# Where plain fp32 products give way to split ones in the up projection of a mixture-of-experts kernel

## The chip, the cores and the metric

The kernel runs on one core of a Trainium2 chip. The metric is the device time of one execution in microseconds. Three executions took 1799.08, 1800.51 and 1802.31 us; their median is 1800.51 us. The profiled execution took 1802.38 us, of which the span from the first to the last instruction is 1800.6 us.

## The reference

The reference is one transformer block over 512 tokens of width 1024: a normalisation, one wide input projection, windowed attention, an RWKV7 recurrence, an output projection, and then the part that matters here, a feed-forward layer with 16384 experts ("PEER"). Each token picks 16 experts in each of 8 heads; the two factors of an expert's number are found by top-16 searches over 128 keys each.

```python
idx = jnp.take_along_axis(cidx, pos, axis=-1)
gate = jax.nn.softmax(top, axis=-1)
def expert_block(args):
    xc, ic, gc = args
    hpre = jnp.einsum('ckd,cd->ck', u_tab[ic], xc).astype(f32)
    act = jax.nn.gelu(hpre, approximate=False) * gc
    return jnp.einsum('ck,ckd->cd', act.astype(v_tab.dtype), v_tab[ic])
```

## The kernel before, in words

For three quarters of the tokens (`TD` = 384) the kernel does not gather experts. It runs all 16384 of them densely, in 128 steps of 128 experts: an up step multiplies the 1024 x 128 slice of the table `u_t` with the 384 normalised tokens and takes the GELU, a matrix of gates (zero for experts that were not picked) is multiplied on, and a down step multiplies with `v_t`. The last 128 tokens gather their rows instead. Matrices are fp32. A product of fp32 accuracy is made in one of two ways. The split way (`mm3`, lines 95 to 98) keeps each operand as a high part of type fp32r and a low part, the rest, and issues three TensorE products: low x high, high x low, high x high. The plain way issues one product of fp32 type, which the trace records as two PE instructions.

The parts of the weights come from `weights` (lines 128 to 141): a DMA on SP's queue into one of `RAWB` = 4 buffers `wraw`, a copy to fp32r on ScalarE (line 139) into `wh` or `wxh`, and a subtraction that gives the low part `wl` or `wxl` on the engine in `lo` (line 140). Each of the four names has two buffers. For the up steps here `lo` is GpSimd (POOL), since `LOP` and `LOQ` are both 4.

The first 42 up steps (`AHEAD`) do not stand in the main loop. They fill TensorE while the top-16 searches and the gates are made, in the function `window`. There PE and VectorE (DVE) follow an order written out by hand; ACT, POOL and SP are ordered by the framework's planner. DVE makes, for each of 48 groups of 8 tokens, one-hot matrices (`onehots`, line 556, output `ot`, 5 buffers) and gated ones (lines 562 and 564, `hi` and `ot`; in every third group ACT does the second of these, line 568), and between the groups pieces of the top-16 search (MAX8, FIND_INDEX8, MATCH_REPLACE8 and small operations, lines 654 to 756). PE makes the gates of a group two groups behind (`gates`, line 581), which frees that group's `ot`. Between the groups PE takes "units" of up steps: `U(n)` advances by `n` of the eight k-parts of a step. 12 units (`RES`) are held back until after the last gates. Then the main loop begins: down step e beside up step e + 42.

An up step has eight k-parts of 128 rows. In the first `PLAIN` steps the parts 0 to 3 are split and the parts 4 to 7 are plain: the raw weights are read by PE directly from `wraw`, against `x2f`, the unsplit tokens, which `whole` builds once in the four buffers of `wxh` and `wxl`. After that all parts are split, and `wxh` and `wxl` carry weights.

```python
def u_prep(e):
    if e < PLAIN:
        U[e] = [weights(a["u_t"][e][:, :4], lo=G)]
        with tc.high_priority(offset=PRE):
            U[e].append(ws.tile([P, 4, P], F32, name="wraw", bufs=RAWB))
            nc.sync.dma_start(U[e][1], a["u_t"][e][:, 4:])
        return
    odd[0] = True
    U[e] = [weights(a["u_t"][e][:, h * 4:h * 4 + 4], lo=G if e <= AHEAD and (2 * e + h) % LOP < LOQ else V) for h in range(2)]
...
            if e < PLAIN and k >= 4:
                PE.matmul(o, uu[1][:, k % 4], x2f[k][:, :TD], start=False, stop=k == KD - 1)
            else:
                uh, ul = uu[k // 4]
                mm3(o, uh[:, k % 4], ul[:, k % 4], x2h[:, k, :TD], x2l[:, k, :TD], k == 0, k == KD - 1)
```

Of the kernel before, what the change touches and what calls it, by code (L numbers as in the profile page):

```python
# [43 lines left out]
AHEAD = 42  # L44
# [6 lines left out]
UN0 = ((14, (1,)), (14, (1,)), (14, (1,)), (14, ()))  # L51
NG8 = TD // 8
GSC = 2.0 ** 15
PLAIN = AHEAD - 2
GB2 = 2
LAG = 2
RES = 12
# [251 lines left out]
def peer(tc, a, out, dump, mm3, split, mhalf, ws, ps, weights, x2h, x2l, xg, h1_dram, dram, hb, qst, tst, tk, tk0, scores,  # L309
# [6 lines left out]
    with ExitStack() as st:  # L316
# [15 lines left out]
# [10 lines that stand above are left out]
        def u_mm(e):  # L342
            uu = U.pop(e)
            o = ps.tile([P, TD], F32, name="mm", bufs=2)
            for k in range(KD):
                if e < PLAIN and k >= 4:
                    PE.matmul(o, uu[1][:, k % 4], x2f[k][:, :TD], start=False, stop=k == KD - 1)
# [1114 lines left out]
```

## Time and profile before

| | value |
|---|---|
| median of 3 executions | 1800.51 us (1799.08 to 1802.31) |
| profiled execution | 1802.38 us |
| its span | 1800.6 us |
| mean granted TensorE clock | 0.98 |
| PE busy | 1719.2 us (95%) |
| DVE busy | 1385.5 us (77%) |
| POOL busy | 786.5 us (44%) |
| ACT busy | 716.6 us (40%) |
| up steps ahead, first plain product to last | 628 to 875 us |
| main loop at full TensorE use | from about 912 us |

The shares are means over stages that are bound by different engines; what a change in one stage is worth is read from the waits of that stage. A matmul's recorded duration overlaps the next one's, so its cost is read from the distance between starts. "L140" is line 140 of the kernel; for a helper like `weights` the tile names tell which use is meant.

### The profile page before, as it was taken

Reading aid. Unit: us, or ns where it says so; the run is one execution under the profiler, and the core shown is the slowest. Engines: PE = TensorE matmul, PEld = TensorE weight load, DVE = VectorE, ACT = ScalarE, POOL = GpSimd, SP = SyncE. Lnnn points to the kernel's source line nnn. Section 1 sums busy time; section 2 is a strip of 40 time slices with the busy share of each in tenths; the row PEclk is TensorE's granted clock in tenths of the full one; section 3 lists DMA queues with packets and bytes.
Section 4 is the critical chain, followed back from the end, with each engine's and each line's share of the span. In section 5 each row is a group of like instructions: output and inputs, shape, how many; then the busy total and the mean of one; then the engine's idle time right before and its main releaser. Section 6 shows DMA issues by size and latency. Waiting matters only on the chain. (4 is left out here: it accounts for less than half of the span.)

```text
span 1800.6 us, 30100 instructions
## 1 busy us (share of the span) xinstructions
PE 1719.2 (95%) x10913; PEld 1433.8 (80%) x10913; DVE 1385.5 (77%) x2540; ACT 716.6 (40%) x1540; POOL 786.5 (44%) x642
## 2 busy tenths in 40 slices
PE   7998899999999889999899999999999999999998
PEld 6766666667778867777789999999999999987886
DVE  4666765755435998998769988787888998989896
ACT  4453132221334545766633333334333333333334
POOL 5534332311154522222255555555555655556550
PEclk9998999999999999999999999999999999999999
DMA  6221111111564324455599999999999999989974
GB/s 209 79 66 46 31 42 48 42 48 48 160 216 134 106 82 177 177 208 206 205 307 320 315 329 328 306 327 325 315 314 332 312 316 332 310 301 299 299 237 161
DMA packets 193397, 378.98 MB, mean 210 GB/s; under 512 B 18624, under 2 KB 65472, under 8 KB 190176
## 3 DMA queue, kind: packets, MB, share of 16 engines
q1 hardware_dynamic: 97344, 175.71, 28.7%
q0 software_dynamic: 36864, 134.23, 22.0%
q10 hardware_dynamic: 59040, 67.12, 11.1%
q8 instruction: 85, 1.39, 0.3%
q14 instruction: 64, 0.52, 0.1%
HBM read 342.12 MB, written 33.55 MB: 209 GB/s over the span
## 5 line engine op out<-in xcount | busy, mean ns | idle before, releaser
L140 POOL TENSOR_TENSOR wl<-wraw,wh 128x512 fp32r<-128x512 f32 (+1 forms) x102 | 146.0, 1432 | 352.5 <-ACT wh L139 304.1
L96 PE MATMUL w<-vh,al 128*128 128x512 f32 x663 | 259.5, 391 | 5.6 <-DVE al L102 5.6
L97 PE MATMUL w<-vl,ah 128*128 128x512 f32 x663 | 259.0, 391 | 0.0
L98 PE MATMUL w<-vh,ah 128*128 128x512 f32 x663 | 258.8, 390 | 0.0
L404 POOL DMA_INDIRECT grow<-v_t,idxV x128 | 172.2, 1345 | 181.0 <-DVE gacc L421 157.2
L404 POOL DMA_INDIRECT grow<-u_rows,idxU x128 | 166.6, 1302 | 178.1 <-DVE grow L411 162.3
L357 ACT ACTIVATE big<-mm 128x384 f32<-128x384 f32 x128 | 62.5, 489 | 422.8 <-PE mm L98 339.9
L96 PE MATMUL mm<-x2h,wl 128*128 128x384 f32 (+1 forms) x544 | 194.7, 358 | 16.0 <-ACT big L357 14.6
L140 DVE TENSOR_TENSOR wl<-wraw,wh 128x512 fp32r<-128x512 f32 x96 | 136.2, 1418 | 95.0 <-ACT wh L139 73.0
L98 PE MATMUL mm<-x2h,wh 128*128 128x384 f32 (+1 forms) x544 | 183.1, 337 | 0.0
L97 PE MATMUL mm<-x2l,wh 128*128 128x384 f32 (+1 forms) x544 | 182.9, 336 | 0.0
L139 ACT ACTIVATE wh<-wraw 128x512 fp32r<-128x512 f32 (+1 forms) x198 | 123.6, 624 | 145.2 <-PE mm L776 50.7
L421 DVE SCALAR_TENSOR_TENSOR gacc<-grow,act,gacc 128x1024 f32<-128x1024 f32 x127 | 166.8, 1314 | 2.2
L102 DVE TENSOR_TENSOR vl<-vraw,vh 128x512 fp32r<-128x512 f32 x212 | 143.1, 704 | 19.3 <-ACT vh L101 19.2
L411 DVE SCALAR_TENSOR_TENSOR grow<-grow,xg 128x1024 f32<-128x1024 f32 x128 | 149.9, 1213 | 0.0
L96 PEld LDWEIGHTS w<-vh,al 128*128 128x128 f32 x663 | 124.9, 188 | 31.1 <-DVE al L102 8.0
L98 PEld LDWEIGHTS w<-vh,ah 128*128 128x128 f32 x663 | 124.7, 188 | 26.3
L370 POOL TENSOR_TENSOR big<-big,gt 128x384 f32<-128x384 f32 x128 | 136.2, 1067 | 20.4 <-ACT gt L586 14.7
L97 PEld LDWEIGHTS w<-vl,ah 128*128 128x128 f32 x663 | 124.9, 188 | 22.6
L101 ACT ACTIVATE vh<-vraw 128x512 fp32r<-128x512 f32 x212 | 127.4, 624 | 37.9 <-DMA vraw<-v_t 29.5
L140 POOL TENSOR_TENSOR wxl<-wraw,wxh 128x512 fp32r<-128x512 f32 (+1 forms) x58 | 83.3, 1436 | 131.4 <-ACT wxh L139 119.0
L96 PE MATMUL mm<-x2h,wxl 128*128 128x384 f32 (+1 forms) x384 | 127.3, 331 | 0.0
(404 smaller groups left out, 4088.8 us busy)
## 6 DMA issues: line engine op xcount, KB each, us to landing
wraw<-u_t SPq DMA_DIRECT2D x256, 256.0 KB
vraw<-v_t SPq DMA_DIRECT2D x212, 256.0 KB
g_dram<-stg ACTq DMA_DIRECT2D x24, 1024.0 KB
gt<-g_dram ACTq DMA_DIRECT2D x60, 384.0 KB
wraw<-wz SPq DMA_DIRECT2D x72, 256.0 KB
wraw<-v_t SPq DMA_DIRECT2D x44, 256.0 KB
wraw<-wq SPq DMA_DIRECT2D x32, 256.0 KB
wraw<-wproj SPq DMA_DIRECT2D x16, 256.0 KB
```

What stands on the lines that cost most here:

```text
L96: PE.matmul(o, ll, rh, start=start, stop=False)
L97: PE.matmul(o, lh, rl, start=False, stop=False)
L98: PE.matmul(o, lh, rh, start=False, stop=stop)
L101: S.activation(hi, src, AF.Copy)
L102: V.tensor_sub(lo, src, hi.bitcast(F32))
L139: S.activation(wh[:, :, :m], raw[:, :, :m], AF.Copy)
L140: lo.tensor_sub(wl[:, :, :m], raw[:, :, :m], wh[:, :, :m].bitcast(F32))
L357: S.activation(H[e], o, AF.Gelu)
L370: G.tensor_mul(ht, ht, g[:, :, e % E2B, :])
L404: G.indirect_dma_start(out=r, out_offset=None, in_=src, in_offset=bass.IndirectOffsetOnAxis(ap=idx[:, i:i + 1], axis=0))
L411: V.scalar_tensor_tensor(r, r, 1.0, xg, op0=ALU.mult, op1=ALU.mult, accum_out=hpre[:, s:s + 1])
L421: V.scalar_tensor_tensor(gacc, r, act[:, i:i + 1], gacc, op0=ALU.mult, op1=ALU.add)
```

## The change

The number of up steps with plain products for half of their contraction falls from 40 (`AHEAD - 2`) to 14. Steps 14 to 39 make all eight k-parts split.

```diff
-PLAIN = AHEAD - 2
+PLAIN = 14
```

## Rows read from the trace of the kernel before

**Rows 1.** Busy time by stretch: PE, PEld (weight load), DVE, ACT and POOL in us with the number of instructions, then the granted TensorE clock, the share of the DMA engines, and GB/s. The stretches are up steps 14 to 39, the way into the main loop, and the main loop.

```profile
715.00:875.00 160.00, 154.49 (x1038) 122.06 (x1035) 147.78 (x437) 102.78 (x241) 40.45 (x28) 0.99 0.54 191
875.00:912.00 37.00, 31.69 (x227) 27.13 (x226) 19.57 (x22) 22.39 (x55) 14.09 (x10) 0.91 0.76 259
912.00:1610.00 698.00, 698.00 (x3553) 637.55 (x3552) 594.68 (x772) 257.96 (x514) 386.13 (x316) 1.00 0.93 321
```

**Rows 2.** Who waited for whom between 711 and 888 us: total us, times, longest us.

```profile
ACT wh L139 <- DMA wraw<-u_t: 22.2, 12, 5.3
DVE ot L556 <- PE w L581: 15.2, 6, 5.1
...
PE mm L96 <- ACT big L357: 5.5, 3, 2.8
```

**Rows 3.** DVE in order of time, the one-hot operations that waited (start us, us; the wait before it and what ended it in brackets).

```profile
711.27 1.23 DVE L556 TENSOR_TENSOR ot<-ids,row 128x2048 f16<-128x2048 f16 x1 [5.05 <-PE w L581]
...
739.44 1.23 DVE L556 TENSOR_TENSOR ot<-ids,row 128x2048 f16<-128x2048 f16 x1 [3.29 <-PE w L581]
...
801.82 1.23 DVE L556 TENSOR_TENSOR ot<-ids,row 128x2048 f16<-128x2048 f16 x1 [1.17 <-PE w L581]
...
815.87 1.22 DVE L556 TENSOR_TENSOR ot<-ids,row 128x2048 f16<-128x2048 f16 x1 [1.66 <-PE w L581]
...
830.89 1.22 DVE L556 TENSOR_TENSOR ot<-ids,row 128x2048 f16<-128x2048 f16 x1 [0.44 <-PE w L581]
...
844.73 1.22 DVE L556 TENSOR_TENSOR ot<-ids,row 128x2048 f16<-128x2048 f16 x1 [3.62 <-PE w L581]
```

**Rows 4.** PE in order of time within one up step: the first of six split products in a row, then the first and the last of the four plain products after them (a plain product is recorded as two instructions, x2).

```profile
783.25 0.34 PE L96 MATMUL mm<-x2h,wl 128*128 128x384 f32 x1
...
784.29 0.81 PE L347 MATMUL mm<-wxh,wraw 128*128 128x384 f32 x2
...
786.22 0.81 PE L347 MATMUL mm<-wxl,wraw 128*128 128x384 f32 x2
```

**Rows 5.** All instructions of the line of the plain products: duration ns min/median/max, first and last start.

```profile
L347 PE MATMUL mm<-wxh,wraw x160: 483/486/847, 628.3 to 874.3; 128*128 128x384 f32 x160
...
L347 PE MATMUL mm<-wxl,wraw x160: 485/486/617, 628.9 to 875.0; 128*128 128x384 f32 x160
```

**Rows 6.** ACT in order of time: the GELU that ends up step 13 (the fourteenth of its line).

```profile
714.72 0.47 ACT L357 ACTIVATE big<-mm 128x384 f32<-128x384 f32 x1
```

**Rows 7.** POOL and ACT groups between 711 and 888 us (ACT: 715 to 880): busy us, mean ns of one, idle before and its releaser.

```profile
L140 POOL TENSOR_TENSOR wl<-wraw,wh 128x512 fp32r<-128x512 f32 x27 | 43.5, 1610 | 125.1 <-ACT wh L139 125.1
L140 POOL TENSOR_TENSOR wxl<-wraw,wxh 128x512 fp32r<-128x512 f32 x2 | 4.0, 2002 | 0.0
```

```profile
L139 ACT ACTIVATE wh<-wraw 128x512 fp32r<-128x512 f32 x26 | 16.3, 629 | 26.8 <-DMA wraw<-u_t 20.0 <-PE mm L98 5.0 <-issue 1.7
```

**Rows 8.** DVE groups between 711 and 888 us: busy us, mean ns of one, idle before.

```profile
L556 DVE TENSOR_TENSOR ot<-ids,row 128x2048 f16<-128x2048 f16 x37 | 48.3, 1305 | 15.2 <-PE w L581 15.2
L562 DVE TENSOR_TENSOR hi<-ot,gps 128x1024 f16<-128x1024 f16 x38 | 31.4, 825 | 0.0
L564 DVE TENSOR_TENSOR ot<-ot,gps 128x1024 f16<-128x1024 f16 x26 | 25.7, 987 | 1.0
L723 DVE TENSOR_TENSOR eq<-eq,tfx 128x2048 bf16<-128x2048 bf16 x4 | 6.7, 1672 | 0.3
L662 DVE FIND_INDEX8 ti<-tv,big 128x8 uint32<-128x128 f32 x20 | 5.5, 285 | 0.0
...
L710 DVE TENSOR_TENSOR wd<-sixteen,sh 128x128 uint32<-128x128 uint32 x2 | 1.5, 766 | 0.1
...
L701 DVE TENSOR_TENSOR ge<-gv 128x128 f32<-128x128 f32 x2 | 1.4, 676 | 0.0
```

**Rows 9.** The three heavy DVE lines over the whole span: duration ns min/median/max, first and last start.

```profile
L556 DVE TENSOR_TENSOR ot<-ids,row x48: 1201/1218/2308, 664.9 to 884.2; 128x2048 f16<-128x2048 f16 x48
L562 DVE TENSOR_TENSOR hi<-ot,gps x48: 677/684/1772, 667.1 to 886.7; 128x1024 f16<-128x1024 f16 x48
L564 DVE TENSOR_TENSOR ot<-ot,gps x32: 691/693/1671, 669.6 to 887.4; 128x1024 f16<-128x1024 f16 x32
```

**Rows 10.** POOL and DVE in order of time at two POOL subtractions (741.22 and 729.85 us), and one DVE operation of line 723 with no POOL work beside it.

```profile
741.22 1.27 POOL L140 TENSOR_TENSOR wl<-wraw,wh 128x512 fp32r<-128x512 f32 x1 [3.95 <-ACT wh L139]
```

```profile
741.37 1.67 DVE L564 TENSOR_TENSOR ot<-ot,gps 128x1024 f16<-128x1024 f16 x1
```

```profile
729.85 1.27 POOL L140 TENSOR_TENSOR wl<-wraw,wh 128x512 fp32r<-128x512 f32 x1 [4.32 <-ACT wh L139]
```

```profile
729.84 0.22 DVE L662 FIND_INDEX8 gi<-gv,cand 128x8 uint32<-128x65 f32 x1
```

```profile
750.43 1.22 DVE L723 TENSOR_TENSOR eq<-eq,tfx 128x2048 bf16<-128x2048 bf16 x1
```

**Rows 11.** The end of the stage in order of time: DVE's last gated operation and its next one, PE's last held-back unit and the first down product.

```profile
887.42 0.69 DVE L564 TENSOR_TENSOR ot<-ot,gps 128x1024 f16<-128x1024 f16 x1
897.56 0.56 DVE L102 TENSOR_TENSOR wl<-big,wh 128x384 fp32r<-128x384 f32 x1 [9.45 <-ACT wh L101]
```

```profile
896.47 0.34 PE L98 MATMUL mm<-x2h,wxh 128*128 128x384 f32 x1
898.27 0.47 PE L96 MATMUL w<-wh,wl 128*128 128x512 f32 x1 [1.46 <-DVE wl L102]
```

## The prediction

> **What bounds the kernel now.** I read the busy time by stretch first. In the main loop PE is busy for all of its 698 us [rows 1]: whatever shifts the start of that loop shifts the end of the kernel by as much, and nothing in the change reaches into the loop. So the question is only when the stage before it ends. In the stretch of up steps 14 to 39 two engines are nearly full: PE with 154.5 of 160 us and DVE with 147.8 [rows 1]. The reader should see that neither share settles which one sets the pace.
>
> The waits come next. DVE's only idle time is before the one-hot operation L556, and PE's gate products end it: 15.2 us in six waits [rows 2]. In time order one wait, at 711.27 us, lies before step 14 begins (step 13's GELU is at 714.72 [rows 6]); the five after it make 3.29 + 1.17 + 1.66 + 0.44 + 3.62 = 10.2 us [rows 3]. PE in turn waits 5.5 us for GELUs that stand behind other work in ACT's queue [rows 2]. So today PE is a little slower than DVE, with DVE running ahead until its five `ot` buffers are used up, and DVE has 10.2 us in hand over the whole stretch. After 844.73 DVE never waits again, and PE's last gates follow DVE's last operation, at 887.42 [rows 11]. That is the balance which the change moves, from both sides.
>
> **What it takes from PE.** The six split products from 783.25 to 784.29 take 1.04 / 6 = 0.173 us each, so a split k-part takes 0.520; the plain ones from 784.29 to 786.22 take 1.93 / 3 = 0.643 us each [rows 4]. 320 records at two for a product are 160 products, 40 steps of four [rows 5]; the change turns 26 x 4 = 104 of them. PE gives back 104 x 0.123 = 12.8 us.
>
> The Trainium skill (FP8 and Floating Point Precision, section TensorE Precision Notes) says that a true fp32 product makes four passes over the array. As an estimate from that page, three passes for four would give back a quarter of 0.643 for each product, 16.7 us; the starts in the trace give 12.8, and the measured number stands.
>
> **What it adds.** Each of the 26 steps gets a second conversion on ACT and a second subtraction on POOL. ACT: 26 x 0.629 = 16.4 us [rows 7], on 102.8 busy of 160 [rows 1]. POOL: 26 x 1.61 = 42 us [rows 7], on 40 busy of 160, so POOL itself stays far from full. The DMAs stay: the same 256 KB are loaded by another line. Raw buffers come free after the subtraction instead of after the last plain product, so ACT's 22.2 us of waiting for raw loads [rows 2] can only shrink. `wxh` and `wxl` become free at the end of step 13 instead of 39; the first conversion into them has the four split parts of step 14 (2.1 us) and a group's gates as cover, and one late start would cost 1 to 2 us of PE, which has 12.8 to give.
>
> ACT works in order, and behind an added conversion stand GELUs (they free PE's accumulators) and gate evictions. From below this costs nothing, because PE's gain covers it; from above, all 16.4 us appear in PE, which with 12.8 us returned would be 3.6 us later than now. I take nothing: DVE, as follows, is later than that.
>
> **What POOL's subtraction does to DVE.** This is the term that decides. At 741.22 a POOL subtraction runs 1.27 us, and beside it the L564 operation takes 1.67 us [rows 10] against a median of 0.693 [rows 9]; the one at 729.85 runs beside FIND_INDEX8, which keeps its 0.22 us [rows 10]. Operations with two tensors are held up; searches are not. The longest cases are 2308 - 1218, 1772 - 684 and 1671 - 693 ns [rows 9], so one meeting costs DVE 0.98 to 1.09 us.
>
> How often do they meet? The sums over 711 to 888 us answer without counting [rows 8]: L556 37 x (1.305 - 1.218) = 3.2 us over its median, L562 38 x (0.825 - 0.684) = 5.4, L564 26 x (0.987 - 0.693) = 7.6, L723 4 x (1.672 - 1.22) = 1.8 (its undisturbed 1.22 is in [rows 10]), and L710 and L701, two each, against 0.28 for an undisturbed one (an estimate: 2 x 0.766 less one meeting of 0.98, halved), 2 x 0.49 + 2 x 0.40 = 1.8. Together 19.8 us, and in that stretch POOL made 27 + 2 = 29 such subtractions [rows 7]: 0.68 us of DVE for each. At the same rate the 26 added ones cost DVE 26 x 0.68 = 17.7 us. From below the cost is zero (all fall beside searches), from above 26 x 1.09 = 28.3 (none does). I take 17.7: the added subtractions are of the same shape in the same stretch.
>
> The Trainium skill (SBUF — State Buffer, section Who interferes with whom) says that GpSimd and a DVE operation with two SBUF inputs lock each other out for a whole instruction, and that one-input operations are spared. The second half agrees with the FIND_INDEX8 at 729.84. By the first, as an estimate, a meeting would cost the 1.27 us of a subtraction and the sum would be 22.9 us; the trace shows 0.98 to 1.09, and it decides.
>
> **The sum.** DVE's list of work is unchanged, in its written order. From 711.27 to its last operation it loses its waits (-10.2 us; PE is 12.8 us faster and DVE later, so its buffers will be free) and gains 17.7: it ends 7.5 us later. PE then waits for DVE; its 12.8 us turn into idle time. From DVE's last operation to the first down product at 898.27 there are 10.9 us [rows 11]: the last gates, 12 held-back units, the eviction and gating of step 0. None of that changes, so the main loop starts 7.5 us later. On the profiled execution's 1802.38 us this is 1809.9; that one lies 1.9 above the median of 1800.51, so the prediction is **1808.0 us**. The likeliest case's own range is 1804 to 1813, from 0.53 to 0.87 us a subtraction.
>
> **Rivals.**
> *PE stays the pace, and the kernel is faster.* Place: DVE's waits before L556. If the added subtractions fall mostly beside searches, they cost DVE less than the time that it has in hand. It decides from 10.2 / 26 = 0.39 us a subtraction downward. For it: 729.85; searches stand in blocks. Against it: 0.68 is the mean of 29 of the same kind. At zero cost PE's gain is the limit: at the wait of 739.44 only four steps have passed (26 steps in 160 us), 4 x 0.49 = 2.0 us, and the 6.9 us of DVE's waits behind it go too, 8.9 us in all and 1791.6. At half the threshold, 26 x 0.2 = 5.2 us, the gain is 5.0 and the time 1795.5. The fewer passes of the page on precision named above point this way.
> *They cancel.* Between 0.39 and 0.53 us a subtraction the end moves by 0 to 3.6 us: 1802 in the middle. For it: the planner may release POOL's pairs together, right after an eviction, at times other than now.
> *ACT's queue becomes the bound.* 16.4 us more in an in-order queue that already made PE wait 5.5 us [rows 2], behind operations that wait for a later DVE; the evictions come late, the gates too, and DVE waits for `ot` again. If half of the 16.4 us shows on top of the 7.5, the time is 1816. Against it: PE now has 12.8 + 7.5 us of slack.
>
> **How the numbers follow.** A measurement of this kernel can tell about 0.2%, 3.6 us, from no change. The forecast gets 0.61, ACT's queue 0.07, cancelling 0.19, PE's pace 0.13. That is slower 0.68, same 0.19, faster 0.13. The range must leave out no more than 2 in 10: from 1797, which leaves out most of PE's pace, to 1816, above which ACT's queue or a dearer subtraction would be.
>
> **What would show it.** Right: between up step 14 and the main loop the waits of L556 for PE's gates are gone or nearly so, L556, L562, L564 and L723 together exceed their medians by some 37 us instead of 20, and PE shows 15 us or more of new idle time before gates, ended by `hi` or `ot`; PE's busy time there is lower by some 13 us; the 898.27 of the first down product becomes some 906. Wrong: L556 still waits for PE by several us and the first down product is earlier; or DVE's excess stays near 20 us although POOL made 26 more subtractions; or PE's new idle time ends with ACT's GELU; or the main loop, which should keep its length, changes.

## The result, and the profile after

The changed kernel takes 1813.35 us (median of 6 executions, 1807.38 to 1814.58) beside 1801.49 us for the kernel before on the same chip: a ratio of 1.0063, 95% interval 1.0048 to 1.0079. It is slower by 11.9 us where 7.5 were forecast; a second measurement of the same two kernels, told below, gave 10.6. The medians below are over all executions; two runs, e1 and e7, each have one far longer execution among theirs (2761.64 and 6726.56 us), and without it their medians are 1800.32 and 1815.39 us. The profiled execution of the change took 1813.65 us, its span 1811.9.

The busy time by stretch, with the columns of [rows 1]: up steps 14 to 39, the way into the main loop, and the main loop. The last line is the whole stretch from step 14 to the first down product.

```profile
715.00:875.00 160.00, 139.14 (x1081) 131.09 (x1080) 158.28 (x421) 110.75 (x258) 88.17 (x53) 0.94 0.52 185
875.00:923.00 48.00, 43.25 (x304) 38.45 (x303) 30.61 (x40) 29.00 (x71) 13.74 (x11) 0.88 0.62 221
923.00:1621.00 698.00, 698.00 (x3554) 637.53 (x3553) 591.86 (x772) 258.11 (x514) 386.63 (x317) 1.00 0.93 321
...
713.00:909.00 196.00, 172.28 (x1342) 160.86 (x1339) 184.46 (x453) 135.71 (x319) 95.81 (x58) 0.93 0.52 189
```

The main loop is what it was. DVE, 147.8 of 160 us before [rows 1], is now busy for 158.3: nothing is left to it but its list of work. PE has gone from 154.5 to 139.1. So the pace has passed from PE to DVE.

Who waited for whom between 711 and 898 us, with the columns of [rows 2]:

```profile
PE mm L96 <- ACT big L357: 20.2, 6, 8.9
...
DVE ot L556 <- PE w L581: 4.4, 1, 4.4
...
ACT wh L139 <- DMA wraw<-u_t: 2.4, 1, 2.4
...
PE w L581 <- DVE hi L562: 0.7, 1, 0.7
```

DVE's six waits for PE's gates [rows 2, 3] have become one, and that one lies before step 14. ACT's waits for raw loads before `wh` fell from 22.2 us to 2.4. But PE's new waits end with ACT's GELU (L357), 20.2 us against 5.5 before, and hardly at all with `hi`.

The DVE groups between 711 and 898 us, with the columns of [rows 8], and POOL's subtractions under them, with the columns of [rows 7]:

```profile
L556 DVE TENSOR_TENSOR ot<-ids,row 128x2048 f16<-128x2048 f16 x37 | 54.8, 1481 | 4.4 <-PE w L581 4.4
L562 DVE TENSOR_TENSOR hi<-ot,gps 128x1024 f16<-128x1024 f16 x37 | 35.3, 954 | 0.0
L564 DVE TENSOR_TENSOR ot<-ot,gps 128x1024 f16<-128x1024 f16 x25 | 29.9, 1197 | 1.0
L723 DVE TENSOR_TENSOR eq<-eq,tfx 128x2048 bf16<-128x2048 bf16 x4 | 5.8, 1455 | 0.3
...
L727 DVE TENSOR_TENSOR eq<-eq 128x1024 bf16<-128x1024 bf16 x4 | 4.7, 1172 | 0.1
L712 DVE TENSOR_TENSOR sh<-rg,sh 128x128 uint32<-128x128 uint32 x2 | 2.8, 1407 | 0.1
...
L732 DVE TENSOR_TENSOR ge<-ge,gs 128x128 f32<-128x128 f32 x2 | 1.8, 916 | 0.1
L676 DVE CAST tf<-ti 128x256 bf16<-128x256 uint32 x2 | 1.5, 768 | 0.1
```

```profile
L140 POOL TENSOR_TENSOR wl<-wraw,wh 128x512 fp32r<-128x512 f32 x27 | 48.8, 1808 | 55.2 <-ACT wh L139 55.2
L140 POOL TENSOR_TENSOR wxl<-wraw,wxh 128x512 fp32r<-128x512 f32 x28 | 44.5, 1592 | 30.4 <-ACT wxh L139 30.4
```

Over the medians of [rows 9] the three one-hot lines lose 37 x 0.263 + 37 x 0.270 + 25 x 0.504 = 32.3 us. The other lines, each over its undisturbed length (1.22, 0.692, 0.293, 0.292 and 0.294 us), add 0.9 (L723), 1.9 (L727), 2.2 (L712), 1.2 (L732) and 0.9 (L676). That is 39.4 us in place of 19.8, and POOL made 55 subtractions in place of 29: 0.72 us each. From 713.27 us to the last gated operation 41 DVE operations take over 0.15 us longer than the same operation does undisturbed, and a POOL operation runs beside every one of the 41; in the kernel before it is 20 of 20.

DVE in order of time, where an added subtraction first falls among one-hot operations (the first two, from 716.21 us, run mostly beside searches), and at the end; then POOL in the same microseconds (start, us, and the wait before in brackets):

```profile
713.27 1.22 DVE L556 TENSOR_TENSOR ot<-ids,row 128x2048 f16<-128x2048 f16 x1 [4.43 <-PE w L581]
...
724.04 0.68 DVE L562 TENSOR_TENSOR hi<-ot,gps 128x1024 f16<-128x1024 f16 x1
724.75 1.67 DVE L564 TENSOR_TENSOR ot<-ot,gps 128x1024 f16<-128x1024 f16 x1
726.34 2.31 DVE L556 TENSOR_TENSOR ot<-ids,row 128x2048 f16<-128x2048 f16 x1
728.57 1.77 DVE L562 TENSOR_TENSOR hi<-ot,gps 128x1024 f16<-128x1024 f16 x1
...
898.90 0.69 DVE L564 TENSOR_TENSOR ot<-ot,gps 128x1024 f16<-128x1024 f16 x1
```

```profile
723.35 2.51 POOL L140 TENSOR_TENSOR wxl<-wraw,wxh 128x512 fp32r<-128x512 f32 x1 [1.42 <-ACT wxh L139]
725.83 1.73 POOL L140 TENSOR_TENSOR wl<-wraw,wh 128x512 fp32r<-128x512 f32 x1
728.27 1.52 POOL L140 TENSOR_TENSOR wxl<-wraw,wxh 128x512 fp32r<-128x512 f32 x1 [0.71 <-ACT wxh L139]
```

The two engines now take turns: three DVE operations in a row are 1.67, 2.31 and 1.77 us long instead of 0.69, 1.22 and 0.68, 3.16 us for three subtractions.

From 711.27 to the end of its last gate operation at 888.12 DVE took 176.85 us before, 10.18 of them waits over 0.2 us; from 713.27 to 899.59 it now takes 186.33, with no such wait. So the waits went (-10.2) and the work grew by 19.7 us, 0.76 a subtraction: 9.5 us. The other 2.0 us of the profiled pair lie before step 14, where the two kernels run the same code (713.27 against 711.27); in the second profile of the change the same operation starts at 709.37, so these 2 us are not the change's.

### The profile page after: what moved, and what is told of

The parts are those of the page before. It is cut to its first block, busy times and chain, and to the rows that moved or that the text cites. A ratio compares the mean times of both kernels' runs of the same rounds, so it can differ in the third digit from the quotient of the medians.

```text
span 1811.9 us, 30401 instructions
## 1 busy us (share of the span) xinstructions
PE 1710.3 (94%) x11017; PEld 1447.9 (80%) x11017; DVE 1404.0 (77%) x2540; ACT 728.6 (40%) x1566; POOL 833.3 (46%) x668
## 3 DMA queue, kind: packets, MB, share of 16 engines
q10 hardware_dynamic: 59040, 67.12, 10.9%
## 4 chain that ended last, share of the span: by engine, by line
PE 47%; DVE 2%; issue 1%; ACT 0%; POOL 0%; DVEq 0%; POOLq 0%; ACTq 0%
PE w L97 9%; PE w L96 9%; PE w L98 9%; PE mm L96 7%; PE mm L98 7%; PE mm L97 7%; DVE gacc L421 0%; DVE al L102 0%; ACT w L472 0%; DVE gt L471 0%; DVE vl L102 0%; DVE gt L481 0%; DVE wl L102 0%; DVE wxl L102 0%; POOL frs L478 0%
## 5 line engine op out<-in xcount | busy, mean ns | idle before, releaser
L140 POOL TENSOR_TENSOR wl<-wraw,wh 128x512 fp32r<-128x512 f32 (+1 forms) x102 | 151.4, 1485 | 285.5 <-ACT wh L139 237.6
L357 ACT ACTIVATE big<-mm 128x384 f32<-128x384 f32 x128 | 62.5, 488 | 417.6 <-PE mm L98 355.1
L96 PE MATMUL mm<-x2h,wl 128*128 128x384 f32 (+1 forms) x544 | 190.6, 350 | 31.9 <-ACT big L357 30.5
L140 DVE TENSOR_TENSOR wl<-wraw,wh 128x512 fp32r<-128x512 f32 x96 | 128.9, 1342 | 98.4 <-ACT wh L139 79.8
L140 POOL TENSOR_TENSOR wxl<-wraw,wxh 128x512 fp32r<-128x512 f32 (+1 forms) x84 | 125.0, 1489 | 158.3 <-ACT wxh L139 145.9
L96 PE MATMUL mm<-x2h,wxl 128*128 128x384 f32 (+1 forms) x488 | 163.8, 336 | 0.0
L98 PE MATMUL mm<-x2h,wxh 128*128 128x384 f32 (+1 forms) x488 | 162.1, 332 | 0.0
L97 PE MATMUL mm<-x2l,wxh 128*128 128x384 f32 (+1 forms) x488 | 162.1, 332 | 0.0
L102 DVE TENSOR_TENSOR vl<-vraw,vh 128x512 fp32r<-128x512 f32 x212 | 144.9, 713 | 21.2 <-ACT vh L101 19.7
L139 ACT ACTIVATE wxh<-wraw 128x512 fp32r<-128x512 f32 x180 | 112.2, 623 | 91.6 <-PE mm L776 44.4
```

What stands on the lines that cost most here:

```text
L96: PE.matmul(o, ll, rh, start=start, stop=False)
L97: PE.matmul(o, lh, rl, start=False, stop=False)
L98: PE.matmul(o, lh, rh, start=False, stop=stop)
L102: V.tensor_sub(lo, src, hi.bitcast(F32))
L139: S.activation(wh[:, :, :m], raw[:, :, :m], AF.Copy)
L140: lo.tensor_sub(wl[:, :, :m], raw[:, :, :m], wh[:, :, :m].bitcast(F32))
```

## The experiments

In the expectations, theory A is the forecast's: POOL's subtractions lengthen DVE's work, and DVE is the pace. Theory B says that ACT's queue is: the added conversions bring GELUs and evictions late. Measured figures are medians and ratios to the kernel before on the same chip. "Stage" is the time from DVE's 12th one-hot operation (711.27 before) to the end of its last one for the gates, "waits" DVE's idle spells over 0.2 us in it, "work" the rest. Added lines shift the line numbers: L584, L582, L585 are the gates' L581, and L360 and L363 are the GELU's L357. The kernel before took 1799.47 us beside e1 to e4, 1799.91 beside e5 to e8 and 1800.32 beside e9 to e12. Stage, waits and work come from one profiled execution each; the two profiles of the change differ by 0.7 us in the stage.

| run | median us | ratio, 95% interval | stage | waits | work |
|---|---|---|---|---|---|
| before | | | 176.85 | 10.18 | 166.67 |
| change | 1813.35 | 1.0063, 1.0048 to 1.0079 | 186.33 | 0 | 186.33 |
| e5_change_again | 1810.52 | 1.0052, 1.0034 to 1.0070 | 187.04 | 0 | 187.04 |
| e1_no_added_sub | 1800.65 | 1.0003, 0.9985 to 1.0020 | 176.86 | 8.62 | 168.24 |
| e2_no_added_conv | 1808.91 | 1.0040, 1.0027 to 1.0054 | 186.48 | 1.07 | 185.42 |
| e6_products_alone | 1789.04 | 0.9936, 0.9919 to 0.9952 | 165.73 | 1.05 | 164.68 |
| e3_before_plus_sub | 1817.05 | 1.0087, 1.0069 to 1.0105 | 195.04 | 18.29 | 176.75 |
| e4_plain27 | 1805.20 | 1.0033, 1.0021 to 1.0046 | 182.44 | 6.36 | 176.08 |
| e7_sub_on_dve | 1815.78 | 1.0079, 1.0059 to 1.0099 | 188.91 | 9.87 | 179.03 |
| e8_before_gelu_first | 1796.01 | 0.9979, 0.9967 to 0.9990 | 172.76 | 5.36 | 167.40 |
| e9_change_gelu_first | 1811.51 | 1.0067, 1.0049 to 1.0085 | 189.24 | 0 | 189.24 |
| e10_no_sub_gelu_first | 1796.00 | 0.9979, 0.9966 to 0.9992 | 172.11 | 3.41 | 168.70 |
| e11_plain34_gelu_first | 1799.03 | 0.9988, 0.9978 to 0.9998 | 176.76 | 3.99 | 172.77 |
| e12_plain27_gelu_first_act | 1806.12 | 1.0036, 1.0019 to 1.0053 | 180.01 | 7.00 | 173.01 |

### The three parts of the change, one left out at a time

**Without the added subtractions.** The new products and conversions stay; the products read the high part in the low one's place.

```diff
 wh = ...
+if not sub:
+    return wh, wh
...
-U[e] = [weights(..., lo=G if ... else V) for h in range(2)]
+U[e] = [weights(..., lo=G if ... else V, sub=h == 0 or e >= AHEAD - 2) for h in range(2)]
```

> The changed kernel without the 26 added POOL subtractions: in steps 14 to 39 the second half's high part stands in for its low part, so products and ACT conversions stay and the output is not the reference's. Theory A (the subtractions hold up DVE): DVE's excess over its undisturbed durations falls from about 41 to about 20 us in the stage, L556 waits for PE again, and the time drops below the kernel before, to about 1792 us (1788 to 1797), since PE keeps its 12.8 us. Theory B (the added conversions in ACT's in-order queue make the stage longer): the conversions are still there, so the time stays near the changed kernel, 1809 to 1814 us.

The stage is 176.86 us, within 0.01 of before's, and the time is that of before. DVE's work falls by 18.1 us against the change, 0.70 us for each of 26 subtractions: theory A's term. But neither theory's time came: A asked for 1788 to 1797 us, B for 1809 or more. DVE waits again, and PE stands before ACT's GELU. The waits between 710 and 887 us:

```profile
DVE ot L559 <- PE w L584: 13.0, 6, 4.4
PE mm L96 <- ACT big L360: 12.4, 5, 5.6
```

So the 12.8 us of PE were not to be had even with subtractions at no cost.

**Without the added conversions.** The new products and subtractions stay; the second half is subtracted from, and multiplied by, the first half's high part.

```diff
+if hi is not None:
+    lo.tensor_sub(wl[:, :, :m], raw[:, :, :m], hi[:, :, :m].bitcast(F32))
+    return hi, wl
...
+    U[e].append(weights(..., lo=G if ... else V,
+                        hi=U[e][0][0] if h and e < AHEAD - 2 else None))
```

> The changed kernel without the 26 added ACT conversions: in steps 14 to 39 the first half's high part serves the second half too, and POOL subtracts it from the second half's raw weights, so the output is not the reference's; products and subtractions stay. Theory A: as the changed kernel, 1808 to 1815 us, DVE's excess about 40 us, no wait of L556 for PE after step 14. Theory B: the time falls to 1795 to 1802 us and PE's wait for GELUs falls from 20 us to about 5.

The stage is 186.48 us, the change's 186.33, and DVE has one wait, of 1.07 us. Beside late subtractions the conversions cost nothing in this stage. By the medians the run is 9.4 us over the kernel before and the change's repeat 10.6, and the two intervals overlap. Theory B is out by its time and by PE's waits for GELUs, which it had at about 5 us; between 711 and 898 us:

```profile
PE mm L96 <- ACT big L363: 13.7, 2, 10.3
```

The longest is 10.3 us with no added conversion in ACT's queue.

**The new products alone.** Neither conversion nor subtraction for the second half; its raw load stays, and the first half's parts are multiplied.

```diff
+if h and e < AHEAD - 2:
+    with tc.high_priority(offset=PRE):
+        nc.sync.dma_start(ws.tile([P, 4, P], F32, name="wraw", bufs=RAWB), a["u_t"][e][:, 4:])
+    U[e].append(U[e][0])
+    continue
```

> The changed kernel without the 26 added conversions and without the 26 added subtractions: in steps 14 to 39 both parts of the first half serve the second half too (its raw weights are still loaded), so the second half of the weights is left out of the result. Only PE's gain is left. Theory C (the conversions in ACT's queue ate the gain in the run without subtractions): 1789 to 1794 us. Theory D (the gain is lost because GELUs stand in ACT's queue behind operations that wait for DVE, conversions or not): as the kernel before, 1797 to 1802 us, and PE waits 11 us or more for GELUs in the stage.

The time is 1789.04 us, 10.9 less than before, and the stage is 11.1 us shorter. PE's gain is real. The four runs make a square: from the products alone the conversions cost 11.1 us of stage, the subtractions 20.8, and both together 20.6. Whichever is later hides the other. In the products alone DVE is the pace again, with 1.05 us of waits; the subtractions added to them make DVE's work grow by 20.7 us, 0.80 each.

Where the conversions' 11.1 us are without subtractions is read from PE's busy time. The stretch from the 12th one-hot operation to the first down product, for the kernel before, the products alone, and products with conversions; then, in the last kernel, the 15 us around its longest wait for a GELU:

```profile
711.00:898.00 187.00, 177.97 (x1238) 141.99 (x1235) 164.90 (x453) 123.20 (x294) 49.21 (x32) 0.98 0.56 197
```

```profile
712.00:888.00 176.00, 164.26 (x1342) 155.16 (x1340) 163.44 (x454) 121.57 (x293) 48.52 (x32) 0.98 0.58 210
```

```profile
710.00:898.00 188.00, 171.30 (x1340) 161.29 (x1338) 166.88 (x454) 135.85 (x320) 45.95 (x32) 0.94 0.54 197
...
750.00:765.00 15.00, 9.36 (x64) 8.60 (x63) 14.52 (x22) 10.63 (x25) 1.55 (x2) 0.77 0.28 107
```

The products alone take 13.7 us of PE's busy time away. With the conversions PE idles 188 - 171.3 = 16.7 us instead of 11.7, and the same products are busy 7.0 us longer, at a granted clock of 0.94 instead of 0.98. Around the wait for a GELU the clock is 0.77: the wait shows twice, once as idle time and once in the clock behind it.

**The same subtractions, with nothing else changed.** The kernel before, with a subtraction into a scratch tile in steps 14 to 39.

```diff
+if e >= 14:
+    scr = tk.sp.tile([P, 4, P], F32R, name="scr")
+    G.tensor_sub(scr, U[e][1], U[e][0][0].bitcast(F32))
```

> The kernel before (plain products in 40 steps) with 26 more subtractions of 128 x 512 on POOL in steps 14 to 39, whose result nobody reads; the output is the reference's. Theory A: DVE gains about 19.7 us of excess and gives up 10.2 us of waits, so 9.5 us more than before: about 1811 us (1807 to 1814). Theory B: no added conversion, so within 2 us of the kernel before, 1800 to 1803 us.

This one overshoots, for a reason of its own. Between 709 and 904 us:

```profile
ACT wh L139 <- DMA wraw<-u_t: 55.2, 18, 6.1
...
DVE ot L559 <- PE w L584: 22.7, 9, 4.4
...
PE mm L96 <- ACT big L360: 18.1, 7, 5.6
```

The scratch subtraction is one more reader of the raw buffers; ACT waits 55.2 us for raw loads where it waited 22.2 [rows 2]. That this reader is the cause was not tested. DVE's work grew by 10.1 us alone and its waits by 8.1: with PE not relieved, the lateness comes back to DVE as waits. By that growth a subtraction costs DVE 0.39 us here, half of what it costs in the change: 16 of the 54 in the stage met no two-tensor operation or cast of DVE, in the change 9 of 55. So the run doesn't measure the price in the change; it shows that the price depends on when the subtractions run.

### Between and beside

**Thirteen added steps instead of 26.**

```diff
-PLAIN = 14
+PLAIN = 27
```

> 27 plain steps, so 13 steps changed in place of 26. Theory A: 13 x 0.76 = 9.9 us of excess for DVE against the waits of L556 that lie behind the change; from the wait at 739 us on that is 9.9 - 6.9 = 3.0 us, from the one at 802 us on 9.9 - 5.7 = 4.2: about 1805 us (1802 to 1808). Theory B, with the loss in proportion to the added conversions: half of 11.9, 1807.5 us.

DVE's work grows by 9.4 us, 13 x 0.72, and 6.4 us of waits are left. Beside the 1799.47 us measured with it the run is 5.7 us slower, where theory A's 3.0 to 4.2 us would give 1802.5 to 1803.7 and theory B's half 1805.4; the interval is 1803.2 to 1807.8. The run doesn't tell the two apart: it is nearer to B's number, while its stage shows A's account with fewer waits used up (3.8 us) than A had counted.

**The change again, unaltered.**

> The changed kernel unaltered, beside the kernel before on the same chip. Its stage should repeat: no wait of L556 after step 14, DVE's last gated operation 185 to 188 us after the one-hot operation that ends the last wait. The 2 us by which that operation came later in the first profile lie in code that both kernels share; if that is a difference between executions it will not repeat, and the median will lie 8 to 12 us over the kernel before.

The ratio is 1.0052. The stage is 187.04 us, no wait, work 20.4 us over before, 0.78 a subtraction.

**The added subtractions on DVE itself**, after the fifth of the eight k-parts of the step before.

```diff
+U[e] = [weights(..., lo=V if e > AHEAD or h and e < AHEAD - 2 else G,
+                later=later if h and e < AHEAD - 2 else None) for h in range(2)]
...
+if k == 4:
+    while later:
+        later.pop(0)()
```

> The changed kernel with the 26 added subtractions on DVE itself, issued in the middle of the step before. By the port theory a subtraction on POOL costs DVE 0.70 us; on DVE it costs its own 0.62 us (start to start of two such in the main loop's lead-in). So 26 x 0.08 = 2 us less: 1808 to 1812 us, if DVE does not wait for ACT's conversions; 5 us or more above that if it does. By a theory in which POOL's work is harmless the 16 us are simply added: 1825 us or more.

The "port theory" is theory A. The DVE group between 711 and 905 us; then one of these subtractions and the operation after it, in order of time:

```profile
L141 DVE TENSOR_TENSOR wxl<-wraw,wxh 128x512 fp32r<-128x512 f32 x26 | 18.3, 706 | 19.9 <-ACT wxh L139 19.8
...
713.96 0.69 DVE L141 TENSOR_TENSOR wxl<-wraw,wxh 128x512 fp32r<-128x512 f32 x1
714.56 1.22 DVE L565 TENSOR_TENSOR ot<-ids,row 128x2048 f16<-128x2048 f16 x1
```

A subtraction made on DVE is recorded with 0.706 us, but the next operation starts 0.60 us after it, less than one made on POOL costs DVE. 24 of the 26 lie in the stage, and its work grows by 12.4 us, where the change's grows by 19.7 and 20.4. But in DVE's fixed order they also wait for ACT's conversion, 19.8 us in all, half of it before the stage: no gain, and the loss is in the waits.

### Is ACT's queue the bound?

PE's 20.2 us before GELUs were a sign that the prediction had called wrong. The longest of them, in the change, on ACT and PE:

```profile
868.60 2.19 ACT L681 ACTIVATE tfx<-tf 128x512 bf16<-128x512 bf16 x4 [4.33 <-DVE eq L723]
870.69 0.61 ACT L139 ACTIVATE wxh<-wraw 128x512 fp32r<-128x512 f32 x1
871.21 1.06 ACT L584 ACTIVATE stg<-w 128x512 f32<-128x512 f32 x2
872.28 1.28 ACT L357 ACT_TABLE_LOAD   x1
873.57 0.49 ACT L357 ACTIVATE big<-mm 128x384 f32<-128x384 f32 x1
...
874.21 0.66 PE L96 MATMUL mm<-x2h,wl 128*128 128x384 f32 x1 [8.87 <-ACT big L357]
```

The head of ACT's queue (L681) waits 4.33 us for a DVE operation; behind it stand one added conversion, two gate evictions and the load of the GELU's table, and then the GELU on which PE waits. The engine named as releaser is ACT; the one that is late is DVE. Three runs, and two tries for a better version after them, put the GELU ahead in ACT's order:

```diff
+with tc.high_priority(offset=PRE if e < AHEAD else 0):
     S.activation(H[e], o, AF.Gelu)
```

**On the kernel before.**

> The kernel before, with the GELUs of the 42 up steps ahead given a higher priority in the planner, so that they stand earlier in ACT's queue. If PE's waits for GELUs (5.5 us in the stage, 11 us with the two before it) hold the stage up, they go and the time falls by 3 to 8 us, 1792 to 1797. If they are only where DVE's lateness shows, PE waits elsewhere and the time stays 1798 to 1802.

The time is 1796.01 us, faster than both kernels. Its stage begins at 704.22 (711.27 before) and is 4.1 us shorter; PE's waits for GELUs are gone from it. By the medians the gain is 3.9 us; the profiled execution, 1792.81 us, is one of the fastest of this run, so the start of its stage overstates it.

**On the change.**

> The changed kernel with the GELUs of the steps ahead given priority. If DVE sets the pace in the stage, its length from the last wait of L556 to DVE's last gated operation stays 185 to 188 us although PE's wait for GELUs (20 us) shrinks; only the steps before the 14th gain, as in the kernel before with this edit, 3 to 5 us: 1805 to 1809. If PE's waits held the change up, the stage falls to 180 or less and the time to 1802 or less.

Between 705 and 902 us PE no longer waits for GELUs but for DVE:

```profile
PE w L582 <- DVE hi L563: 10.9, 4, 4.6
```

The stage is 189.24 us with no DVE wait, over the 185 to 188 expected, and the median lies over the 1805 to 1809: the change gains nothing from this order. DVE is the pace, and the GELU waits were PE's spare time spent in another place. Theory B falls for the change, and with it the prediction's rival of ACT's queue.

**On the kernel without the added subtractions.**

> The run without the added subtractions, with the GELUs given priority; the low parts of the second halves of steps 14 to 39 are again left out of the result. If the added conversions cost their time by standing ahead of GELUs in ACT's queue, PE's 12.8 us come back: stage 165 to 170 us, 1785 to 1792. If they cost it in another way (late weights), the stage stays 174 to 177 us and the time 1795 to 1799, the gain of the priority alone.

The time is 1796.00 us, that of the kernel before with the same priority: the products' gain is still not there, though between 706 and 880 us no product waits for a GELU. PE and, in the last two lines, ACT in order of time:

```profile
759.00 0.22 PE L585 MATMUL w<-ot 128*128 128x128 f16 x1 [1.75 <-ACT ot L572]
759.06 0.22 PE L585 MATMUL w<-hi,ot 128*128 128x128 f16 x1
759.30 0.22 PE L585 MATMUL w<-ot 128*128 128x128 f16 x1
...
757.49 0.62 ACT L139 ACTIVATE wh<-wraw 128x512 fp32r<-128x512 f32 x1
758.00 0.62 ACT L139 ACTIVATE wxh<-wraw 128x512 fp32r<-128x512 f32 x1
758.52 2.18 ACT L572 ACTIVATE ot<-ot,gpl 128x128 f16<-128x128 f16 x7
```

Here PE's gates follow ACT's own part of the one-hot work (`ot`, line 568 before) at 0.30 us a pair, and that part stands behind two conversions. Over that window PE waits 4.4 us for `ot` and 4.8 us for evictions. So more stands behind conversions than GELUs; how the lost gain divides among GELUs, `ot`, evictions and the clock stays open.

**Two tries for a better version**: 34 plain steps, and 27 with ACT taking its part in every second group (`if i % 2` for `if i % 3`), both with the GELU first.

> 34 plain steps (6 of the 26 changed) with the GELUs given priority. PE gains 6 x 0.49 = 2.9 us, DVE 6 x 0.72 = 4.3 us of work against 5.4 us of waits that it has with the priority alone. Within 2 us of that run's 1796: 1794 to 1798.

> 27 plain steps, GELUs given priority, and ACT makes the low gated product of every second group in place of every third. DVE: 13 x 0.72 = 9.4 us more for subtractions, 8 operations of 0.6 to 1.0 us fewer, so about 3 us more, within its 5.4 us of waits; PE gains 6.4 us; ACT gets 8 x 2.5 = 20 us more. 1790 to 1796 if ACT's queue holds; over 1800 if it does not.

Neither does better than the kernel before with the GELU first, and both lie above what was expected, at 1799.03 and 1806.12 us. With 34 plain steps six more subtractions go with 5.4 us more DVE work, 0.9 each. With 27, DVE's work is 3.1 us less than in the run with 27 alone, but PE follows ACT, and DVE's waits are 7.0 us.

## Why the prediction was right, and where it was not

*What PE gives back.* Right: 13.7 us of busy time and 10.9 us of the kernel's time by the products alone, 12.8 forecast. In the change itself PE's busy time from step 14 on falls only from 177.97 to 172.28 us, by 5.7 where the prediction's sign asked for some 13. The granted clock of the stretch is 0.93 instead of 0.98; that this cost nothing, since PE waited anyway, is an argument and was not tested.

*ACT's conversions at nothing, "because PE's gain covers it".* The value was right for the change (the run without them has the same stage), the reason was half wrong. Without the subtractions the conversions took the whole gain back, 11.1 us of stage. What covered them was DVE's lateness. With that the rival in which PE stays the pace had no ground: subtractions at no cost at all gave 1800.65 us where 1791.6 were named as its limit, and the point of 0.39 us a subtraction from which it was to decide doesn't exist in this kernel: at no cost the kernel is as fast as before, not faster.

*POOL's subtractions at 0.68 us of DVE.* The mechanism is shown by leaving them out. Its size by the growth of DVE's work is 0.76 and 0.78 in the two profiles, 0.70 against the run without them and 0.80 between the products alone and the run without conversions: within the 0.53 to 0.87 of the likeliest case, above its middle. This is the mis-sized term, and it makes the difference in the stage, 19.7 and 20.4 us instead of 17.7. Of the 39.4 us of excess in the change 33.2 are in the four lines that the sign named, for 37 forecast. The dearer places are new: with two subtractions for a step POOL's queue holds the next one ready, so that three DVE operations in a row are held up, and L712, L727, L732 and a CAST are hit that the forecast hadn't listed. The half-sentence of the Trainium skill (SBUF — State Buffer, section Who interferes with whom) on which the forecast let one-input operations go free has its own exception there: casts can take a mode with both ports. The CAST of L676 agrees: 0.294 and 0.293 us before, 0.591 and 0.946 after.

*DVE's waits, -10.2 us.* Right: none is left in step 14 and later.

*The end of the stage.* Right: from DVE's last operation to the first down product 9.77 us (10.15 before), and the main loop has its 698 us. The first down product starts at 909.36, in the second profile at 907.41, for some 906 forecast.

*The sign that failed.* PE's new idle time, 196 - 172.3 = 23.7 us against 9.0, 14.7 more, was to end with `hi` or `ot`, and the prediction listed the GELU as a sign against itself. It ended with the GELU, and the forecast held all the same. The step that failed is the reading of that sign: an engine with spare time shows its wait at the first thing that is late on its path, and in an in-order queue behind a DVE-fed operation that is the GELU. Two runs told the theories apart: without added conversions PE still waited 13.7 us for GELUs and the stage stayed, and with the GELU moved ahead the waits for it went and the stage did not get shorter.

*Sum.* The stage came out 9.5 and 10.2 us longer for 7.5 forecast, the median 11.9 and 10.6 us. What the medians show beyond the stage, 2.4 and 0.4 us, is no larger than the differences between executions of the same code before step 14.

## What to carry to other kernels

Price work moved to GpSimd by what it costs VectorE's two-tensor operations beside it: here 0.7 to 0.8 us of VectorE for each 128 x 512 subtraction, more than the 0.60 us, from start to start, that VectorE needs to make it itself. On VectorE, though, it stood in a fixed order and waited for its input. When a change relieves one engine and loads two, run it with each load left out: a load that costs nothing beside the other can take the whole gain alone. A releaser in a table of waits names the last link; look what the head of that engine's queue waited for before calling it the bound.

## What the runs showed of the hardware that was not expected

The clock was low behind the stretches in which PE idled, and this belongs to the price of a late GELU. The changed kernel in slices of 5 us, PE's busy time in the third column and the granted clock in the third from the end:

```profile
753.00:758.00 5.00, 2.06 (x17) 1.74 (x14) 4.93 (x6) 2.90 (x5) 3.21 (x2) 0.92 0.40 145
758.00:763.00 5.00, 0.87 (x3) 0.90 (x4) 4.86 (x8) 4.98 (x10) 0.14 (x1) 0.50 0.19 52
763.00:768.00 5.00, 5.00 (x29) 4.69 (x28) 4.86 (x7) 0.99 (x4) 0.00 (x0) 0.55 0.52 213
768.00:773.00 5.00, 5.00 (x41) 4.84 (x40) 4.79 (x8) 5.00 (x13) 2.62 (x2) 1.00 0.16 54
```

PE was busy for 2.9 of 10 us; then it had work throughout, and at 0.55 the clock was still near its lower level of 1.2 GHz: 29 products in 5 us, and 41 in the next 5 us at 1.00.

A plain fp32 product of 384 columns costs as much as 3.7 of the split way's (0.643 us to 0.173 [rows 4]), and turning 104 of them did shorten the kernel by 10.9 us once nothing had to prepare their operands: in this kernel the price is in the preparation, not on TensorE.
